# A two-layer hybrid decoder step: LayerNorm's subtraction on one engine, the recurrent state without its turn, far attention scores in residue order, and longer bank times in the plan of the passes

## The chip, the cores and the metric

The kernel runs on one core of one Trainium2 chip. The metric is the device time of one execution in microseconds (us). A core has TensorE (PE, matrix products, with its weight loads shown as PEld), VectorE (DVE), ScalarE (ACT), GpSimd (POOL) and SyncE (SP, which here only issues DMA transfers). Matrix products write to PSUM, which is used here as eight banks of 128 partitions x 512 float32 values; the other engines read it from there.

## The reference, cut to what matters

Two layers are applied to a prompt of 1024 positions and to 8 single decode positions. Each layer projects its input, splits the columns into an attention part (8 heads) and a recurrent RWKV-7 part (8 heads), joins both, and ends in two LayerNorms around a feed-forward part:

```python
def layer_norm(x, g, b):
    mu = xf.mean(-1, keepdims=True)
    var = jnp.square(xf - mu).mean(-1, keepdims=True)
    return (xf - mu) * lax.rsqrt(var + LN_EPS) * g + b

p   = x @ w_in
att = dilated_attention(q, k, v)       # (window, dilation) = (128,1), (512,4), (2048,16)
S   = S*w_t + (S @ a_t) b_t + v_t k_t  # RWKV-7 state, one step per position; y_t = S @ r_t
x1  = layer_norm(ALPHA*x + concat(att, rwk) @ w_out)
y   = layer_norm(ALPHA*x1 + square(relu(x1 @ w_up)) @ w_down)
```

The prompt's attention needs, for far keys, only positions whose distance is a multiple of 4. Outputs are the two results, the shifted rows, the final states, and the keys and values. All of it is float32.

## The kernel before

The prompt is worked on in two halves of 512 positions per layer; the second half carries the 8 decode columns too. A weight matrix product is computed as three products of a high and a low part (`dense_steps`, L389 to L391), each weight tile being split by ACT (L362) and DVE (L363).

The order of PE's instructions is written out ahead of time by a planner, `Streams`. Each stream is a generator that yields (cost, bank and how long it is held, latency until the next piece, bank it needs). The streams are, in order of priority, `s2` (the recurrence, `stage2`), `norm` (`normed`), `s1` (`stage1`), `att` (`attention`), `post`, `kv`, and last `dense`. In planned time, the first stream that is ready takes the next piece; `dense` fills the rest, and once entered it keeps PE for a while (`RUN`). The eight PSUM banks are divided by tag: `r` 1, `o` 2, `d` 3 (dense), `a` 2. The planned times decide the order alone: on the chip, semaphores decide. Other engines than PE keep an order that the framework makes.

**LayerNorm.** The last matrix product ahead of a LayerNorm (`out2` at L946, `down` at L1023) is computed in `passes`: eight row blocks o for the first 256 columns, then eight for the rest. A block is 12 matmuls of 256 columns, then DVE adds the bank into `t` (L952, L1028), and `ln.add` gathers sums and squares on DVE and POOL. `finish` (L750) makes the mean (L755), subtracts it from eight tiles at L759 (tiles 3 and 7 on DVE, the other six on POOL), makes the variance (L762, DVE at L763), and takes the inverse root on ACT. `scale` multiplies on DVE (L778). The first 256 columns are finished during the second eight blocks, the rest during the work that follows. There are 16 finishes. The last one ends the run.

**Recurrence.** `stage2` works on a unit of 256 positions of one pair of heads as four chunks; there are 32 units. After small solves it forms, per half c, products with `Pt` (L1365) and, over 128 rows, with `TV` (L1370: 64-column weights, 128 columns read). Then the chunks run in sequence: the incoming state `Z` is multiplied with `FG` (L1384, 128 columns), the part that is the new state is copied to `St` by DVE (L1386), turned by a product with a stacked identity (L1391, bank `r`), and scaled into the next `Z` by DVE (L1393). Each of these is a piece of its own.

**Gate.** `normed` makes the group norm of a unit in three pieces of tag `o`; where the decode columns come along (8 units), a further small product `pgd` (L1423) takes a bank of its own between the first and the second.

**Attention.** `att_load` stages q and k in two rotating buffers `stg` (L1544); ACT casts them (L1564, L1568) and POOL subtracts for the low parts (L1565, L1569). In the second half `qf` and `kf` are transferred straight from DRAM (L1556, L1557). `attention` computes for each of four query tiles and two heads the far scores (L1596) as four products, one per residue c, of 64 rows, 32 weight columns and 128 read columns; both operands are taken with a step of four elements. Then come the near scores (L1607, L1608).

Of the kernel before, what the change touches and what calls it, by code (L numbers as in the profile page):

```python
# [21 lines left out]
NB = 8  # L22
# [6 lines left out]
HB = T // 2  # L29
# [18 lines left out]
SWITCH = 280  # L48
SLK = (1.2, 2.2)
# [217 lines left out]
def body(ctx, tc, I, O):  # L267
# [130 lines left out]
    def dense(items, kts, xhh, xll, evac):  # L398

        res = []  # L400
        yield (0, None, 0, "d")
        yield from dense_steps(items, kts, xhh, xll, res)
        for it, p in zip(items, res):
            r = evac(it, p)
            if r is not None:
                yield r
        for i, it in enumerate(items):
            yield (res[-1] if i == 0 else 0, ("d", 900 + 500 * i), 0, None)
# [310 lines left out]
    class LayerNorm:  # L719
# [30 lines left out]
        def finish(self, c0, n, wait=0, spread=0):  # L750
            l, c = self.l, slice(c0, c0 + n)
            cm, s1, s2 = self.cm[:, c], self.s1[:, c], self.s2[:, c]
            yield (0, None, wait, "d")
            pm = bank("d", "lnm")
            PE.matmul(pm[:, :n], ones, s1, start=True, stop=True)  # L755
            A.activation(cm, pm[:, :n], AF.Copy, scale=1.0 / D)
            A.activation(s1, pm[:, :n], AF.Square, scale=1.0 / D)
            for k in range(8):
                (V if k % 4 == 3 else G).tensor_tensor(self.t[:, k, c], self.src(k, c0, n), cm, op=ALU.subtract)  # L759
            yield (860 * n / 512, ("d", 1300), 0, "d")  # L760
            pq = bank("d", "lnq")
# [104 lines left out]
    def half(l, h, prev=None):  # L866
# [82 lines left out]
        def out2(o, w, c0, nn):  # L949
            def ev(it, p):  # L950
                _, _, c0, n = it
                evs.append(V.tensor_tensor(src(o, c0, n), p[:, :n], src(o, c0, n), op=ALU.add))  # L952
            return dense([(w, 128, c0, nn)], K4, *acc(hs), ev)
# [70 lines left out]
        def down(o, w, c0, nn):  # L1024
            def ev(it, p):
                _, _, c0, n = it
                to = t[:, o, c0:c0 + n]
                evs.append(V.tensor_tensor(to, p[:, :n], to, op=ALU.add))  # L1028
            return dense([(w, 128, c0, nn)], K4, *acc(hs), ev)
# [281 lines left out]
    def stage2(l, h, p, u, s, st, Z, Zp):  # L1311
# [45 lines left out]
        for c in range(2):  # L1357
            pb = bank("o", f"pO{c}")
            o3 = pb.rearrange("p (b x) -> p b x", b=2)
            Oc.append(o3)  # L1360
            r = slice(64 * c, 64 * c + 64)
            for tb in range(2):
                for hd in range(2):
                    hs = slice(64 * hd, 64 * hd + 64)
                    PE.matmul(o3[hs, tb, 0:128], Pt[r, hd * 2 + tb, :], LB[r, hd, 2 * tb + c, 64 * c:64 * c + 128],  # L1365
                              start=(tb == 0), stop=True, skip_group_check=True)
            for tb in range(2):
                for hd in range(2):
                    hs = slice(64 * hd, 64 * hd + 64)
                    PE.matmul(o3[hs, tb, 128:256], TV[:, 2 * tb + c, hd, 0, :], LB[:, hd, 2 * tb + c, 64 * c:64 * c + 128],  # L1370
                              start=False, stop=True, skip_group_check=True)
            F4 = FG.rearrange("p (b c) x -> p c b x", c=2)[:, c]
            f0, g0 = 64 * (1 - c), 64 * c
            V.tensor_tensor(F4[:, :, f0:f0 + 64], AR[:, :, 320 * c:320 * c + 64], o3[:, :, f0:f0 + 64], op=ALU.subtract)
            V.tensor_tensor(F4[:, :, g0:g0 + 64], bc(istk, [(0, 2), (1, 64)]), o3[:, :, g0:g0 + 64], op=ALU.subtract)
            yield (960, None, 0 if c == 0 else 900, None if c == 0 else "r")
        note("lb", s)
        for cc in range(4):
            tb, c = divmod(cc, 2)
            o3 = Oc[c]  # L1380
# [31 lines left out]
    def normed(l, h, p, u, s, gup, gs):  # L1412
# [7 lines left out]
        if h == 1 and u == NU - 1:  # L1420
# [3 lines left out]
            V.tensor_copy(dd["gsd"][:, p, :], pz[:, 0:8])  # L1424
# [5 lines left out]
        pb = bank("o", "pgv")  # L1430
        PE.matmul(pb[:, 0:256], C("blk"), sq, start=True, stop=True)
# [103 lines left out]
    def att_load(l, h, p):  # L1535
# [39 lines left out]
    def attention(l, h, p, ops, vT, ahead):  # L1575
# [5 lines left out]
        for j in range(4):  # L1581
# [5 lines left out]
            Es = []  # L1587
            mx = ap_.tile([128, 12], F32, tag="mx", bufs=2, name="mx")
            for hd in range(2):
                hs = slice(64 * hd, 64 * hd + 64)  # L1590
                E = ap_.tile([128, 640], F32, tag="E", bufs=2, name="E")
                pS = bank("a", "pS")
                i, o = 2 * hd, 0
                if h == 1:
# [3 lines left out]
                    u0 = 32 * (7 - qt)  # L1598
                    far = (E[:, 0:128], pS[:, 0:128], C("far")[:, u0:u0 + 128], 1.0, -3e38, ALU.add, ALU.max,
                           mx[:, i:i + 1])  # L1600
                    i, o = i + 1, 128
                    if w > 384:
                        V.tensor_tensor_reduce(*far)
                        yield (300, ("a", 700), 0, "a")
                        pS, o = bank("a", "pS"), 0
                n = max(w, 256)
                PE.matmul(pS[:, o:o + n], qS[hd][:, ql:ql + 128], kS[hd][:, 128 * k0:128 * k0 + n], start=True, stop=False)  # L1607
                PE.matmul(pS[:, o:o + n], qL[hd][:, ql:ql + 128], kS[hd][:, 128 * k0:128 * k0 + n], start=False, stop=True)  # L1608
                if o > 0:
                    V.tensor_tensor_reduce(*far)  # L1610
# [3 lines left out]
                yield (n * 0.9 + 2.3 * o, ("a", 500 + w * 1.1 + o), 0, "a")  # L1614
# [5 lines left out]
                Es.append(E)  # L1620
# [282 lines left out]
```

## Time and profile before

| What | us |
|---|---|
| Median of three executions | 3280.85 (3280.17 to 3285.87) |
| Profiled execution, its own time | 3282.56 |
| Its span, first to last instruction | 3280.7 |
| PE busy in the span | 3130.2 |
| DVE, ACT, POOL busy | 2064.6, 1445.1, 983.3 |

The span is what the trace shows; the execution's own time lies 1.9 us above it. Mean granted clock of TensorE is 0.983 of its full 2.4 GHz. In the rows below a matmul on float32 operands stands as two records, so a count of 512 is 256 products. "Idle before" is the time in which an engine had nothing to do ahead of an instruction, with what ended it.

### The profile page before, as it was taken

The numbers are of one execution on the slowest core, as the hardware profiler recorded it, in microseconds if no ns is written. First come the engines' busy times: TensorE is split into PE (matmuls) and PEld (weight loads), VectorE is DVE, ScalarE is ACT, GpSimd is POOL, SyncE is SP. The second block draws the span as 40 slices with busy tenths as digits, with TensorE's granted clock in tenths as the row PEclk, the third lists the DMA queues.
The fourth block names the chain that finished last, engine by engine and source line by source line (L and its number), as shares of the span: only waits on it lengthen the run. The fifth ranks groups of instructions, "written<-read, shape, count | busy, mean of one in ns | idle before, by whom it ended". The sixth has DMA issues, their size and how long they took to land. (4 is left out here: it accounts for less than half of the span.)

```text
span 3280.7 us, 65951 instructions
## 1 busy us (share of the span) xinstructions
PE 3130.2 (95%) x24732; PEld 2656.7 (81%) x24732; DVE 2064.6 (63%) x4703; ACT 1445.1 (44%) x3266; POOL 983.3 (30%) x1841
## 2 busy tenths in 40 slices
PE   9999999899999999999999999998999999899998
PEld 7768887777777787788999999877767777889997
DVE  5666667855557476677665576568655664875556
ACT  4445454544433364454443345444434333543334
POOL 1443335521221134463121122456121201620012
PEclk9999999999999999999999999999999999999999
DMA  7544445344343355533333236543343434423332
GB/s 230 153 136 128 129 136 164 85 124 126 111 114 103 98 157 164 157 102 105 89 96 90 89 96 185 152 133 100 97 119 106 119 107 125 135 82 91 94 89 83
DMA packets 370503, 393.58 MB, mean 120 GB/s; under 512 B 145816, under 2 KB 223080, under 8 KB 370184
## 3 DMA queue, kind: packets, MB, share of 16 engines
q10 hardware_dynamic: 121152, 213.44, 22.0%
q1 hardware_dynamic: 249032, 175.93, 18.9%
q8 instruction: 195, 3.19, 0.4%
q14 instruction: 124, 1.02, 0.1%
HBM read 325.30 MB, written 63.97 MB: 119 GB/s over the span
## 5 line engine op out<-in xcount | busy, mean ns | idle before, releaser
L389 PE MATMUL dps<-xh,wh 128*128 128x256 f32 (+3 forms) x2984 | 974.1, 326 | 14.9 <-ACT wh L362 6.5
L390 PE MATMUL dps<-xl,wh 128*128 128x256 f32 (+3 forms) x2984 | 947.7, 318 | 11.0 <-DVE xl L781 8.0
L391 PE MATMUL dps<-xh,wl 128*128 128x256 f32 (+3 forms) x2984 | 943.8, 316 | 1.7 <-DVE wl L363 1.6
L362 ACT CAST wh<-wr 128x512 fp32r<-128x512 f32 (+1 forms) x772 | 474.6, 616 | 818.2 <-PE dps L390 759.5
L363 DVE TENSOR_TENSOR wl<-wr,wh 128x512 fp32r<-128x512 f32 (+1 forms) x772 | 579.5, 751 | 357.1 <-ACT wh L362 335.9
L389 PEld LDWEIGHTS dps<-xh,wh 128*128 128x128 f32 x2984 | 567.6, 190 | 75.9 <-issue 18.1
L390 PEld LDWEIGHTS dps<-xl,wh 128*128 128x128 f32 x2984 | 567.7, 190 | 49.1 <-DVE xl L781 12.2
L391 PEld LDWEIGHTS dps<-xh,wl 128*128 128x128 f32 x2984 | 567.4, 190 | 40.5 <-DVE wl L363 3.9
L389 PE MATMUL dps<-hh,wh 128*128 128x512 f32 (+2 forms) x1600 | 527.5, 330 | 9.1 <-ACT lnm L731 3.9
L390 PE MATMUL dps<-hl,wh 128*128 128x512 f32 (+2 forms) x1600 | 513.5, 321 | 3.5 <-DVE mx L1615 1.5
L391 PE MATMUL dps<-hh,wl 128*128 128x512 f32 (+2 forms) x1600 | 512.8, 321 | 0.0
L389 PEld LDWEIGHTS dps<-hh,wh 128*128 128x128 f32 x1600 | 304.4, 190 | 42.5 <-issue 9.6
L390 PEld LDWEIGHTS dps<-hl,wh 128*128 128x128 f32 x1600 | 304.7, 190 | 24.9 <-DVE hl L852 2.8
L391 PEld LDWEIGHTS dps<-hh,wl 128*128 128x128 f32 x1600 | 304.3, 190 | 22.9
L1234 POOL TENSOR_TENSOR tm<-BL,XB 32x15 f32<-32x15 f32 (+7 forms) x480 | 146.7, 306 | 394.2 <-DMA BL<-d_el 348.6
L995 DVE TENSOR_TENSOR t<-dps,t 128x256 f32<-128x256 f32 (+1 forms) x240 | 123.7, 516 | 165.3 <-PE dps L391 164.6
L1236 POOL TENSOR_TENSOR XB<-XB,tm 32x15 f32<-32x15 f32 (+7 forms) x480 | 156.6, 326 | 34.6
L748 POOL TENSOR_TENSOR ln<-ln,lsq 128x256 f32<-128x256 f32 (+1 forms) x112 | 90.8, 811 | 247.4 <-ACT lsq L746 243.4
L963 DVE CAST hh<-rl 128x256 fp32r<-128x256 f32 (+2 forms) x200 | 73.8, 369 | 96.3 <-ACT rl L962 93.2
L737 POOL TENSOR_TENSOR t<-t,ln 128x256 f32<-128x256 f32 (+1 forms) x32 | 27.8, 904 | 350.3 <-ACT ln L731 350.3
L961 ACT ACTIVATE rl<-dps 128x256 f32<-128x256 f32 (+2 forms) x200 | 88.3, 442 | 97.1 <-PE dps L391 90.5
L389 PE MATMUL dps<-hh,xh 128*128 128x256 f32 (+1 forms) x368 | 110.0, 299 | 13.2 <-DVE t L1028 5.8
(345 smaller groups left out, 5080.4 us busy)
## 6 DMA issues: line engine op xcount, KB each, us to landing
wr<-in_w_ff_up ACTq DMA_DIRECT2D x272, 256.0 KB
wr<-in_w_ff_down ACTq DMA_DIRECT2D x256, 256.0 KB
wr<-in_w_in ACTq DMA_DIRECT2D x220, 256.0 KB
stg<-d_qkv SPq DMA_DIRECT2D x128, 128.0 KB
wr<-in_w_out ACTq DMA_DIRECT2D x64, 256.0 KB
z<-d_z SPq DMA_DIRECT2D x24, 384.0 KB
d_qkv<-qe SPq DMA_DIRECT2D x128, 64.0 KB
kvc<-in_cache_k SPq DMA_DIRECT2D x32, 256.0 KB
```

The costliest lines, as they stand in the source:

```text
L362: self.copies.append(A.copy(h[:, :, :m], w[:, :, :m]))
L363: V.tensor_tensor(lo[:, :, :m], w[:, :, :m], h.bitcast(F32)[:, :, :m], op=ALU.subtract)
L389: PE.matmul(p[:m, :n], wh[:, wk % 4, :m], hi, start=(i == 0), stop=False)
L390: PE.matmul(p[:m, :n], wh[:, wk % 4, :m], lo, start=False, stop=False)
L391: PE.matmul(p[:m, :n], wl[:, wk % 4, :m], hi, start=False, stop=(i == last))
L737: G.tensor_tensor(t, t, self.cm[:, c0:c0 + n], op=ALU.subtract)
L748: G.tensor_tensor(s2, s2, sq, op=ALU.add)
L961: A.activation(r, p[:, :n], AF.Relu)
L963: V.tensor_copy(hh[:, c0:c0 + n], r)
L995: V.tensor_tensor(to, p[:, :n], to, op=ALU.add)
L1234: G.tensor_tensor(tv, bc(BL[:, 17 * j + 1:17 * j + 2], [(1, m), (0, j + 1)]), bc(XB[:, 16 * j:16 * j + 1], [(0, m), (1, j + 1)]), op=ALU.mult)
L1236: G.tensor_tensor(xv, xv, tv, op=ALU.add)
```

## The change

It has six parts. (1) `finish` subtracts the mean from all eight tiles on DVE. (2) `dense` takes the time that it holds a bank in the plan as an argument, and `out2` and `down` pass 2400 ns for the first column block and 4500 for the second in place of 900. (3) `stage2` computes the products with `TV` and `Z` in two halves of 64 columns; in one of them the operands trade places, so that the new state comes out turned already, and copy, turn and their bank are left out. The two halves c become one piece. (4) `normed` puts the decode columns' product in the third piece's bank. (5) `att_load` stages `qf` and `kf` through `stg`, and POOL copies them in residue order. (6) `attention` reads them side by side and makes the far scores of both heads together, alternating between the heads, in two banks.

```diff
+HOLD = (2400, 4500)
-    def dense(items, kts, xhh, xll, evac):
+    def dense(items, kts, xhh, xll, evac, hold=900):
...
-            yield (res[-1] if i == 0 else 0, ("d", 900 + 500 * i), 0, None)
+            yield (res[-1] if i == 0 else 0, ("d", hold + 500 * i), 0, None)
...
             for k in range(8):
-                (V if k % 4 == 3 else G).tensor_tensor(self.t[:, k, c], self.src(k, c0, n), cm, op=ALU.subtract)
+                V.tensor_tensor(self.t[:, k, c], self.src(k, c0, n), cm, op=ALU.subtract)
...
-            return dense([(w, 128, c0, nn)], K4, *acc(hs), ev)
+            return dense([(w, 128, c0, nn)], K4, *acc(hs), ev, HOLD[c0 > 0])
...
+        for c in range(2):
+            o3, f0, g0 = Oc[c], 64 * (1 - c), 64 * c
             for tb in range(2):
                 for hd in range(2):
                     hs = slice(64 * hd, 64 * hd + 64)
-                    PE.matmul(o3[hs, tb, 128:256], TV[:, 2 * tb + c, hd, 0, :], LB[:, hd, 2 * tb + c, 64 * c:64 * c + 128],
+                    PE.matmul(o3[hs, tb, 128 + f0:192 + f0], TV[:, 2 * tb + c, hd, 0, :], LB[:, hd, 2 * tb + c, 64:128],
+                              start=False, stop=True, skip_group_check=True)
+                for hd in range(2):
+                    hs = slice(64 * hd, 64 * hd + 64)
+                    PE.matmul(o3[hs, tb, 128 + g0:192 + g0], LB[:, hd, 2 * tb + c, 2 * g0:2 * g0 + 64], TV[:, 2 * tb + c, hd, 0, :],
                               start=False, stop=True, skip_group_check=True)
...
-            yield (960, None, 0 if c == 0 else 900, None if c == 0 else "r")
+        yield (1920, None, 900, None)
...
-                    PE.matmul(o3[hs, tb, 128:256], Z[hs, :], FG[hs, cc, :], start=False, stop=True, skip_group_check=True)
-            St = rp.tile([128, 64], F32, tag="St", bufs=2, name="St")
-            V.tensor_copy(St, o3[:, tb, 128 + 64 * c:192 + 64 * c])
-            yield (280, None, 900, "r")
-            pz = bank("r", "pz")
-            for hd in range(2):
-                hs = slice(64 * hd, 64 * hd + 64)
-                PE.matmul(pz[hs, 0:64], St[hs, :], istk[hs, :], start=True, stop=True)
+                    PE.matmul(o3[hs, tb, 128 + g0:192 + g0], FG[hs, cc, g0:g0 + 64], Z[hs, :], start=False, stop=True,
+                              skip_group_check=True)
+                for hd in range(2):
+                    hs = slice(64 * hd, 64 * hd + 64)
+                    PE.matmul(o3[hs, tb, 128 + f0:192 + f0], Z[hs, :], FG[hs, cc, f0:f0 + 64], start=False, stop=True,
+                              skip_group_check=True)
...
-            V.tensor_scalar(Z, pz[:, 0:64], Wd[:, cc, 64:65], None, op0=ALU.mult)
+            V.tensor_scalar(Z, o3[:, tb, 128 + g0:192 + g0], Wd[:, cc, 64:65], None, op0=ALU.mult)
             if cc < 3:
-                yield (130, ("r", 650), 900, None)
+                yield (280, None, 1000, None)
...
-            yield (860, ("o", 1000), 0, "o")
-            pz = bank("o", "pgd")
-            PE.matmul(pz[:, 0:8], gup, gs[:, UN:UN + NB], start=True, stop=True)
...
         pb = bank("o", "pgv")
+        if h == 1 and u == NU - 1:
+            PE.matmul(pb[:, 256:256 + NB], gup, gs[:, UN:UN + NB], start=True, stop=True)
...
-            S.dma_start(qf, d_qkv[l][1][p, 0])
-            S.dma_start(kf, d_qkv[l][0][p, 1])
+            for f, src, dst, at in ((qf, d_qkv[l][1][p, 0], inrow, byres),
+                                    (kf, d_qkv[l][0][p, 1], lambda t: t.rearrange("p (c k) -> p c k", c=4),
+                                     lambda t: t.rearrange("p (k c) -> p c k", c=4))):
+                t = ap_.tile([128, HB], F32, tag="stg", bufs=2, name="stg")
+                S.dma_start(t, src)
+                AQ.tensor_scalar(dst(f), at(t), 1.0, None, op0=ALU.mult)
...
-                    for c in range(4):
-                        PE.matmul(pS[32 * c:32 * c + 32, 0:128], qf[hs, ql + c:ql + 128:4], kf[hs, c:HB:4],
-                                  start=True, stop=True)
...
+                pSs = [bank("a", "pS") for _ in range(2)]
+                for c in range(4):
+                    for hd in range(2):
+                        hs = slice(64 * hd, 64 * hd + 64)
+                        PE.matmul(pSs[hd][32 * c:32 * c + 32, 0:128], qf[hs, ql + 32 * c:ql + 32 * c + 32],
+                                  kf[hs, 128 * c:128 * c + 128], start=True, stop=True)
```

## Rows read from the trace of the kernel before

**Rows 1.** The page's busy table: engine, busy us (share of span) xinstructions.

```profile
PE 3130.2 (95%) x24732; PEld 2656.7 (81%) x24732; DVE 2064.6 (63%) x4703; ACT 1445.1 (44%) x3266; POOL 983.3 (30%) x1841
```

**Rows 2.** Waits of PE: waiter <- releaser: us in total, times, longest us.

```profile
PE pgd L1423 <- ACT gs L1426: 11.3, 6, 4.1
...
PE pz L1391 <- DVE St L1386: 8.2, 3, 6.7
```

**Rows 3.** PE in order of time from 179.6: start, length in us, instruction.

```profile
179.62 0.39 PE L390 MATMUL dps<-xl,wh 128*128 128x512 f32 x1
179.85 0.40 PE L391 MATMUL dps<-xh,wl 128*128 128x512 f32 x1
180.18 0.33 PE L1391 MATMUL pz<-cst,St 64*64 64x64 f32 x4
180.44 0.50 PE L389 MATMUL dps<-xh,wh 128*128 128x512 f32 x1
180.78 0.39 PE L390 MATMUL dps<-xl,wh 128*128 128x512 f32 x1
```

**Rows 4.** Stretches: length, busy us of PE, PEld, DVE, ACT, POOL; clock, DMA.

```profile
1143.00:1179.00 36.00, 31.08 (x225) 28.98 (x225) 32.91 (x65) 21.83 (x51) 18.07 (x24) 0.95 0.31 90
2244.00:2290.00 46.00, 42.34 (x381) 37.70 (x380) 38.23 (x90) 19.58 (x49) 28.52 (x56) 0.93 0.24 66
```

**Rows 5.** PE's groups by line: xrecords | busy us, mean ns | idle us before.

```profile
L1391 PE MATMUL pz<-cst,St 64*64 64x64 f32 x512 | 43.0, 246 | 8.2 <-DVE St L1386 8.2
L1596 PE MATMUL pS<-kf,qf 64*32 64x128 f32 x512 | 42.9, 413 | 0.1
```

**Rows 6.** PE in order of time, the last turn that stands alone.

```profile
2685.90 0.33 PE L1391 MATMUL pz<-cst,St 64*64 64x64 f32 x4
```

**Rows 7.** PE in order of time, the product with the incoming state.

```profile
128.71 0.44 PE L1384 MATMUL pO<-FG,Z 64*64 64x128 f32 x4
129.08 0.44 PE L1607 MATMUL pS<-kS,qS 128*128 128x384 f32 x1
```

**Rows 8.** PE in order of time, the attention's far product with v.

```profile
510.32 0.64 PE L1662 MATMUL pof<-FT,vT 128*64 128x64 f32 x16
510.89 0.39 PE L389 MATMUL dps<-xh,wh 128*128 128x256 f32 x1
```

**Rows 9.** PE in order of time, the recurrence's local product.

```profile
119.00 0.66 PE L1370 MATMUL pO<-LB,TV 128*64 128x128 f32 x8
119.59 0.66 PE L1630 MATMUL pET<-cst,E 128*128 128x128 f32 x4
```

**Rows 10.** PE in order of time, the far scores and the decode's product.

```profile
442.34 0.67 PE L1596 MATMUL pS<-kf,qf 64*32 64x128 f32 x8
442.94 0.39 PE L1607 MATMUL pS<-kS,qS 128*128 128x256 f32 x1
...
857.04 0.64 PE L1818 MATMUL pdo<-kvc,dsc 128*32 128x128 f32 x16
857.62 0.50 PE L389 MATMUL dps<-xh,wh 128*128 128x512 f32 x1
```

**Rows 11.** Waits of ACT and POOL at the staged tiles; POOL's subtraction, ns min/median/max.

```profile
ACT kS L1568 <- DMA stg<-d_qkv: 44.9, 23, 4.1
...
POOL qL L1565 <- ACT qS L1564: 85.7, 23, 14.4
...
L1565 POOL TENSOR_TENSOR qL<-stg,qS x32: 1524/1556/1851, 84.8 to 2553.0; 128x512 fp32r<-128x512 f32 x32
```

**Rows 12.** DVE in order of time, the last finish.

```profile
3269.38 1.32 DVE L759 TENSOR_TENSOR t<-t,ln 128x264 f32<-128x264 f32 x2 [1.76 <-ACT ln L756]
...
3272.15 4.65 DVE L778 SCALAR_TENSOR_TENSOR t<-t,par,ln 128x264 f32<-128x264 f32 x8 [1.11 <-ACT ln L766]
```

**Rows 13.** DVE by line: durations in ns min/median/max, first and last start.

```profile
L747 DVE TENSOR_TENSOR ln<-ln,t x84: 405/427/4503, 592.7 to 3267.2; 128x256 f32<-128x256 f32 x66, 128x264 f32<-128x264 f32 x18
...
L778 DVE SCALAR_TENSOR_TENSOR t<-t,par,ln x128: 464/482/1030, 613.8 to 3276.3; 128x256 f32<-128x256 f32 x96, 128x264 f32<-128x264 f32 x32
```

More of the change, by code (lines that the diff above doesn't have):

```diff
@@ L1028, in ev @@
                 evs.append(V.tensor_tensor(to, p[:, :n], to, op=ALU.add))
-            return dense([(w, 128, c0, nn)], K4, *acc(hs), ev)
+            return dense([(w, 128, c0, nn)], K4, *acc(hs), ev, HOLD[c0 > 0])
         yield from passes(down, ln)
@@ L1357, in stage2 @@
         for c in range(2):
-            pb = bank("o", f"pO{c}")
-            o3 = pb.rearrange("p (b x) -> p b x", b=2)
+            o3 = bank("o", f"pO{c}").rearrange("p (b x) -> p b x", b=2)
             Oc.append(o3)
@@ L1369, in stage2 @@
                     hs = slice(64 * hd, 64 * hd + 64)
-                    PE.matmul(o3[hs, tb, 128:256], TV[:, 2 * tb + c, hd, 0, :], LB[:, hd, 2 * tb + c, 64 * c:64 * c + 128],
+                    PE.matmul(o3[hs, tb, 128 + f0:192 + f0], TV[:, 2 * tb + c, hd, 0, :], LB[:, hd, 2 * tb + c, 64:128],
[3 more added lines that the diff above has]
+                    PE.matmul(o3[hs, tb, 128 + g0:192 + g0], LB[:, hd, 2 * tb + c, 2 * g0:2 * g0 + 64], TV[:, 2 * tb + c, hd, 0, :],
                               start=False, stop=True, skip_group_check=True)
             F4 = FG.rearrange("p (b c) x -> p c b x", c=2)[:, c]
-            f0, g0 = 64 * (1 - c), 64 * c
             V.tensor_tensor(F4[:, :, f0:f0 + 64], AR[:, :, 320 * c:320 * c + 64], o3[:, :, f0:f0 + 64], op=ALU.subtract)
             V.tensor_tensor(F4[:, :, g0:g0 + 64], bc(istk, [(0, 2), (1, 64)]), o3[:, :, g0:g0 + 64], op=ALU.subtract)
-            yield (960, None, 0 if c == 0 else 900, None if c == 0 else "r")
+        yield (1920, None, 900, None)
         note("lb", s)
@@ L1379, in stage2 @@
             tb, c = divmod(cc, 2)
-            o3 = Oc[c]
+            o3, f0, g0 = Oc[c], 64 * (1 - c), 64 * c
             if Z is not None:
@@ L1419, in normed @@
         V.scalar_tensor_tensor(y, pb[:, 0:256], -1.0 / 64, y, op0=ALU.mult, op1=ALU.add)
-        if h == 1 and u == NU - 1:
-            yield (860, ("o", 1000), 0, "o")
-            pz = bank("o", "pgd")
-            PE.matmul(pz[:, 0:8], gup, gs[:, UN:UN + NB], start=True, stop=True)
-            V.tensor_copy(dd["gsd"][:, p, :], pz[:, 0:8])
         gg = gs[:, 0:256]
@@ L1430, in normed @@
         pb = bank("o", "pgv")
+        if h == 1 and u == NU - 1:
+            PE.matmul(pb[:, 256:256 + NB], gup, gs[:, UN:UN + NB], start=True, stop=True)
+            V.tensor_copy(dd["gsd"][:, p, :], pb[:, 256:256 + NB])
         PE.matmul(pb[:, 0:256], C("blk"), sq, start=True, stop=True)
@@ L1586, in attention @@
             ql = j * 128
-            Es = []
+            Es, pSs, far = [], [], []
             mx = ap_.tile([128, 12], F32, tag="mx", bufs=2, name="mx")
             for hd in range(2):
[L1590 to L1594, printed above, removed]
-                    for c in range(4):
-                        PE.matmul(pS[32 * c:32 * c + 32, 0:128], qf[hs, ql + c:ql + 128:4], kf[hs, c:HB:4],
-                                  start=True, stop=True)
[L1598 to L1606, printed above, removed]
+                Es.append(ap_.tile([128, 640], F32, tag="E", bufs=2, name="E"))
@@ new lines, in attention @@
+            if h == 1:
+                yield (0, None, 0, ("a", 2))
+                pSs = [bank("a", "pS") for _ in range(2)]
+                u0 = 32 * (7 - qt)
+                for c in range(4):
[3 more added lines that the diff above has]
+                                  kf[hs, 128 * c:128 * c + 128], start=True, stop=True)
+                for hd in range(2):
+                    far.append((Es[hd][:, 0:128], pSs[hd][:, 0:128], C("far")[:, u0:u0 + 128], 1.0, -3e38, ALU.add, ALU.max,
+                                mx[:, 2 * hd:2 * hd + 1]))
+                if w > 384:
+                    for hd in range(2):
+                        V.tensor_tensor_reduce(*far[hd])
+                    yield (0, ("a", 700), 0, None)
+                    yield (300, ("a", 900), 0, "a")
+                    pSs, far = [], []
@@ L1607, in attention @@
+            n = max(w, 256)
+            o = 128 if far else 0
+            for hd in range(2):
+                E, i = Es[hd], 2 * hd + h
+                pS = pSs[hd] if far else bank("a", "pS")
                 PE.matmul(pS[:, o:o + n], qS[hd][:, ql:ql + 128], kS[hd][:, 128 * k0:128 * k0 + n], start=True, stop=False)
                 PE.matmul(pS[:, o:o + n], qL[hd][:, ql:ql + 128], kS[hd][:, 128 * k0:128 * k0 + n], start=False, stop=True)
-                if o > 0:
-                    V.tensor_tensor_reduce(*far)
+                if far:
+                    V.tensor_tensor_reduce(*far[hd])
@@ L1613, in attention @@
                                        mx[:, i - 1:i] if h else -3e38, ALU.add, ALU.max, mx[:, i:i + 1])
-                yield (n * 0.9 + 2.3 * o, ("a", 500 + w * 1.1 + o), 0, "a")
+                yield (n * 0.9 + 1.2 * o, ("a", 500 + w * 1.1 + o), 0, "a" if hd == 0 and not far else None)
                 V.tensor_scalar(mx[:, 4 + hd:5 + hd], mx[:, i:i + 1], -0.125, None, op0=ALU.mult)
@@ L1619, in attention @@
                 V.tensor_scalar(E[:, :f + w], E[:, :f + w], mx[:, 8 + hd:9 + hd], None, op0=ALU.mult)
-                Es.append(E)
             if j == 3:
```

## The prediction

> **What bounds the kernel now.** I read the busy table first. TensorE (PE) is busy 3130.2 of the 3280.7 us span, VectorE (DVE) 63%, and GpSimd (POOL) 30% [rows 1]. So PE is the bound, and there are two ways to gain: give it less to do, or end one of its waits, which together are 3280.7 - 3130.2 = 150 us. The view of who waited for whom says how these are spread. The largest entry is 11.3 us in six waits, and the one for the state's copy, 8.2 in three, comes a few lines down [rows 2]. The reader should see that no single wait carries the run.
>
> A PE row's length is not its price, since matmuls overlap. The price is the distance from one start to the next, read from the time-ordered PE rows. Dense rows of 512 columns follow each other in 0.23 us. Around a small group the distance grows. Before the turn of the state at 180.18 it is 0.33 (179.85 to 180.18), and after the turn the first dense row holds 0.34 (180.44 to 180.78) [rows 3]. So one trip from dense work to small work and back costs about 0.10 + 0.11 = 0.2 us beside the small work itself.
>
> Last I read the table by stretches for the LayerNorm passes. In the pass at 1143 only dense work runs, and DVE is busy 32.91 of 36.00 us, PE 31.08. There DVE sets the pace. In the pass at 2244 other streams fill in (381 matmul records against 225), and PE idles 46.00 - 42.34 = 3.7 us [rows 4]. Going by the code and the record counts, three of the eight passes are of the second kind, so about 11 us of idle time lie in them.
>
> **The change part by part.** The sum is made against the profiled execution, 3282.56 us (span 3280.7 and 1.9 around it), which lies 1.7 above the median of 3280.85.
>
> *The state is not turned.* The 512 records of the turn [rows 5] are groups of four (two matmuls, two records each), so 128 groups. Each occupies 0.26 us (180.18 to 180.44) [rows 3]. 128 x 0.26 = -33 us, all of it PE time.
>
> *Fewer pieces.* A unit's tail falls from ten pieces to five. Of the 128 turns, 27 stand alone between dense rows, the first at 180.18 [rows 3], the last at 2685.90 [rows 6]: 27 x 0.2 = -5. The other 101 share their trip with other streams, and up to 101 x 0.2 = 20 could go. I take a quarter, -5, because the other streams' work still has to enter somewhere. Together -10 (bounds -5 and -25).
>
> *The product with the incoming state in halves.* It exists 120 times (128 less the 8 first chunks without a state). Now it is four records of 128 columns in 0.37 us (128.71 to 129.08) [rows 7]. Then it is eight of 64. As two separate groups like the turn's that is 0.52. For a second group that follows at once, the nearest row is the far product with v, whose sixteen 64-column records take 0.57 us (510.32 to 510.89), 0.036 each [rows 8]. 0.26 + 4 x 0.036 = 0.40, so +0.03 x 120 = +4 (bounds: 8 x 0.036 = 0.29, -10; 0.52, +18).
>
> *The local product in halves.* Now it is eight records of 128 columns in 0.59 us (119.00 to 119.59) [rows 9], 64 times. Then it is sixteen of 64 columns with 128 rows and 64 columns of weights, which is the form of rows 8: 0.57. I take 0. The far end is the isolated price of 0.26 for four: 1.04 a time, 64 x 0.45 = +29.
>
> A rule of the Trainium skill speaks against both halvings. TensorEngine Tiling (Array Packing), section Instruction Overhead, gives every matmul about 60 cycles of overhead. By it, as an estimate, 240 + 256 = 496 more matmuls at 25 ns would cost 12 us and the whole sum would be -63. Rows 8 and 9 disagree, since half the columns there cost half the time. Either result lies in the forecast's own range.
>
> *Far scores by residue.* Eight records of 128 columns, read with a step of four, take 0.60 us (442.34 to 442.94). The decode's product, also 32 columns of weights and 128 read columns but side by side, has sixteen in 0.58 (857.04 to 857.62) [rows 10]. That is 0.075 against 0.036 a record. The 512 records [rows 5] at 0.039 less give -20. I take the nearest row's price as it stands. The ends are 0 (the step is not what costs) and -25 (the two heads, on different rows of the array, overlap too).
>
> *What the residue order costs.* Eight loads of q and k (layers x head pairs, second half only) pass two more tiles through the two staging buffers, and POOL copies each. A copy is one input of 128x512; a POOL subtraction of that size took 1.56 us [rows 11]. 16 x 1.56 = 25 us at most on an engine that is busy for a third of the time. But the first q tile's transfer on SyncE's queue now waits for a buffer that POOL must empty, and behind it stand all later loads of that queue. ScalarE (ACT), which casts the tile, waits too, and behind ACT stand weight casts and the relu that PE needs. ACT already waits for staged tiles 23 times, 44.9 us, 4.1 at the longest [rows 11]. I take +5: eight loads, 4 us more each, a sixth of it reaching PE, because the load for the next pair starts well ahead of its first use. Ends: 0, and 8 x 4.1 = +33.
>
> *The gate's last columns ride in the next bank.* The six waits of 11.3 us [rows 2] are for ACT's copy that frees a bank the piece no longer takes. -11 (0 if the wait moves to the next group, where ACT is just as late). The eight groups themselves stay.
>
> *The copy of the state.* Its 128 DVE copies go, and with them the 8.2 us wait [rows 2]. The state's scaling is next in line and inherits part. -4 (bounds -8, and +5 if it is later than the copy was).
>
> *DVE alone subtracts the mean.* At the end of the run two subtractions on DVE, beside POOL's six, take 1.32 us, 0.66 each [rows 12]; DVE's add over the same size in the sum alone has a median of 0.427 [rows 13]. So eight on DVE in a row are 3.4 us instead of 1.32. What follows gains. Eight scalings took 4.65 there, while POOL was still subtracting [rows 12], against a median of 0.482 alone [rows 13], 3.9. At the run's end this chain is all there is: +2.1 - 0.8 = +1.3 us. The other fifteen finishes have the same balance or a better one, and part of it lies under PE work. I take +1 and, for all fifteen, 0. The bounds are 15 x 1.3 = +20 where nothing covers it, and -8 if POOL's freed time helps its other streams.
>
> *Banks held longer in the model.* HOLD changes no instruction, only the planner's order. Above c0 = 0 a bank counts as free 4.5 us after its block. Two blocks of the other banks cover about 2.8 (2 x 12 rows of 256 columns, each at half of the 0.23 us of a 512-column row [rows 3]), so the planner looks for 1.7 us of other work per block. In the three passes with such work, about 11 us of PE idle time can be filled, at one more trip of 0.2 per block (24 blocks, +5). I take -4 (bounds -11 and +5). In the other five passes there is nothing to insert.
>
> *Clock.* In the pass at 2244 the granted clock is 0.93 and at 1143 0.95 [rows 4], that is, some of that time at 1.2 instead of 2.4 GHz, after PE had idled. Fewer waits leave fewer such stretches: -3 (0 to -8).
>
> Sum: -33 - 10 + 4 + 0 - 20 + 5 - 11 - 4 + 1 + 0 - 4 - 3 = -75. From the median, 3280.85 - 75 = **3206 us**.
>
> **The rivals.**
> *Half of it comes back as waits.* PE gets 75 us less to do, but the dense stages then run closer to DVE and ACT, whose work hardly shrinks, and in the passes DVE is already ahead of PE [rows 4]. For it: ACT's and POOL's queues stand in order behind late transfers [rows 11]. Against it: outside the passes DVE has a third of its time free [rows 1]. At half, 3281 - 38 = 3243.
> *More than the sum.* The trips fall by the whole 25, the far scores by 25, the halves at the incoming state by 10, and the fill in the passes by 11: -75 - 15 - 5 - 14 - 7 = -116, 3165. It needs every bound at its good end; halfway, 3185, is more credible.
> *Slower: the staging chain.* POOL is in order. When its copy of the q tile stands behind one of its waits for ACT, the buffer stays full, SyncE's queue stands, ACT waits for the tile and PE for ACT. POOL's waits of this kind reach 14.4 us [rows 11]. Eight loads at 14.4, all passed on to PE, are 115 us: 3206 + 110 (the sum held 5 already) = 3316. It decides from (75 + 5) / 8 = 10 us per load. Against it: no ACT wait for a staged tile was longer than 4.1 [rows 11].
> *The change does not do what it says.* The far scores keep 0.075 a record, and the halves cost what isolated groups cost (+18 + 29 - 4): -75 + 20 + 43 = -12, nearly even, 3269. Within 0.2%, about 6.5 us, it would need a little more, such as the bank wait staying.
>
> **How the numbers follow.** Forecast (3188 to 3226) 0.55; half comes back (3226 to 3262) 0.20; more than the sum (below 3188) 0.14; no gain to speak of (3262 to 3287) 0.06, of which 0.04 within 0.2%; slower 0.05. The time is that of the likeliest, 3206. For 8 in 10 the range takes the forecast, most of the half case and most of the better one: 3172 to 3250. About 0.2% is what a measurement of this kernel can tell from no change. Faster by more 0.91, within it 0.04, slower by more 0.05.
>
> **What would show it.** The turn's records are gone, and eight records of the incoming product lie at 0.40 us. The local product stays at 0.59 for sixteen. Far scores at or below 0.30 per eight. No PE wait stands at the gate's columns. In the pass at 1143 DVE does eight subtractions in 3.4 us and PE's idle time is unchanged; in those with other work it is lower. PE's busy time falls by some 50 to 60 us. What would make it wrong: ACT waits for staged tiles well above 45 us in all, PE waits for weight casts that were not there, small groups priced by count instead of by columns, or a PE idle time that grows as its busy time falls.

## The result and the profile after

The changed kernel took 3236.3 us (median; 3232.2 to 3244.7) against 3280.5 of the kernel before: ratio 0.9866, 95% interval 0.9842 to 0.989. That is 44 us less, where the forecast was 75 less. The direction is right, and the range (3172 to 3250) holds the time, but it lies among the times of the rival that half of the gain comes back as waits (3226 to 3262, given 0.20), and not in the forecast's own range.

The page of the profiled execution (3244.69 us, the slowest of the four, 8 us above their median), span and busy table, as [rows 1]:

```profile
span 3242.9 us, 66797 instructions
...
PE 3054.3 (94%) x25212; PEld 2651.7 (82%) x25212; DVE 2034.9 (63%) x4671; ACT 1439.2 (44%) x3266; POOL 930.1 (29%) x1761
```

Two numbers tell the story. PE's busy time fell by 3130.2 - 3054.3 = 75.9 us. Its idle time rose from 3280.7 - 3130.2 = 150.5 to 3242.9 - 3054.3 = 188.6, by 38.1. The span's 37.8 is the difference. The work went as forecast or better, and the waits gave about half of it back (by the median, which is 44 us less, a little under half).

First the work, PE in order of time in the profile after (start, length, instruction), of the same kinds as [rows 7, 9, 10]:

```profile
118.39 0.68 PE L1365 MATMUL pO<-LB,Pt 64*64 64x128 f32 x16
119.00 0.34 PE L1372 MATMUL pO<-LB,TV 128*64 128x64 f32 x4
...
125.70 0.33 PE L1389 MATMUL pO<-Z,FG 64*64 64x64 f32 x4
125.87 0.28 PE L1393 MATMUL pO<-FG,Z 64*64 64x64 f32 x4
126.08 0.66 PE L1664 MATMUL po<-ET,vT 128*64 128x128 f32 x8
...
249.68 0.34 PE L1372 MATMUL pO<-LB,TV 128*64 128x64 f32 x4 [1.06 <-ACT TV L1354]
...
250.55 0.29 PE L1376 MATMUL pO<-TV,LB 128*64 128x64 f32 x4
250.77 0.66 PE L698 MATMUL pqt<-cst,qe 128*128 128x128 f32 x4
...
435.38 0.45 PE L1603 MATMUL pS<-kf,qf 64*32 64x128 f32 x16
435.76 0.39 PE L1619 MATMUL pS<-kS,qS 128*128 128x256 f32 x1
```

Read the distance from a group's start to the next group's. The product with the state takes 0.38 (125.70 to 126.08), against 0.37 before. The local product takes 1.09 for both halves c (249.68 to 250.77; its first and last rows are shown), against two times 0.59. The far scores of both heads take 0.38, against two times 0.60. The products with `Pt` of both halves take 0.61 (118.39 to 119.00). In the kernel before, one half took 0.58, twice a unit:

```profile
117.25 0.65 PE L1365 MATMUL pO<-LB,Pt 64*64 64x128 f32 x8
117.83 0.66 PE L1370 MATMUL pO<-LB,TV 128*64 128x128 f32 x8
```

Then the waits of PE (in total, times, longest us), as [rows 2]:

```profile
PE dps L391 <- DVE xl L782: 11.9, 20, 1.6
PE pgm L1420 <- ACT y L1401: 11.1, 9, 2.3
PE pET L1641 <- DVE E L1631: 8.8, 3, 6.5
PE pgv L1432 <- ACT gq L1426: 8.7, 3, 4.5
PE pO L1389 <- DVE Z L1396: 8.5, 8, 2.0
...
PE pgv L1432 <- DVE gsd L1431: 5.6, 5, 3.3
```

The first is of dense work and was there before (8.0, at the same place). The five below it are of small pieces. Before, the state's scaling had 5.5, the gate's product (pgv, for gq) 1.4, and the other three did not stand in the list. Summed over PE's groups, idle time fell in dense work from 55.6 to 49.0 us, and rose in the group norm and gate (pgm, pgd, pgv) from 12.7 to 26.6 and in attention from 6.2 to 28.2. The groups of attention (xrecords | busy us, mean ns | idle us before):

```profile
L1641 PE MATMUL pET<-cst,E 128*128 128x128 f32 x336 | 58.7, 291 | 10.0 <-DVE E L1631 8.8 <-DVE bv L1276 0.9 <-ACT TV L1268 0.3
...
L1619 PE MATMUL pS<-kS,qS 128*128 128x256 f32 (+2 forms) x128 | 51.5, 409 | 7.6 <-DVE ao L1666 4.1 <-ACT LB L1256 3.1 <-POOL kS L1574 0.4
...
L1673 PE MATMUL pof<-FT,vT 128*64 128x64 f32 x256 | 11.0, 231 | 4.3 <-ACT FT L1657 4.3
```

With 3.4 at the far scores and 2.9 at the product with v, these make 28 us. Of the 8.8 us at L1641, 6.5 are a single wait, inside the LayerNorm pass at 2229. First PE's row, then three of DVE's ahead of it:

```profile
2274.75 0.69 PE L1641 MATMUL pET<-cst,E 128*128 128x128 f32 x2 [6.51 <-DVE E L1631]
```

```profile
2256.25 1.76 DVE L760 TENSOR_TENSOR t<-t,lnm 128x256 f32<-128x256 f32 x5
...
2262.54 2.16 DVE L779 SCALAR_TENSOR_TENSOR t<-t,par,ln 128x256 f32<-128x256 f32 x4
...
2274.29 0.41 DVE L1631 TENSOR_SCALAR E<-E,mx 128x384 f32<-128x384 f32 x1
```

DVE shows no idle time between 2256 and 2274. The softmax of both heads stands there in line behind LayerNorm's subtractions and scalings and the recurrence's operands, and PE waits for the last step of it.

### The profile page after: what moved, and what is told of

Read it like the earlier page. It is cut to its first block, busy times and chain, and to the rows that moved or that the text cites. A ratio compares the mean times of both kernels' runs of the same rounds, so it can differ in the third digit from the quotient of the medians.

```text
span 3242.9 us, 66797 instructions
## 1 busy us (share of the span) xinstructions
PE 3054.3 (94%) x25212; PEld 2651.7 (82%) x25212; DVE 2034.9 (63%) x4671; ACT 1439.2 (44%) x3266; POOL 930.1 (29%) x1761
## 5 line engine op out<-in xcount | busy, mean ns | idle before, releaser
L1235 POOL TENSOR_TENSOR tm<-BL,XB 32x15 f32<-32x15 f32 (+7 forms) x480 | 156.1, 325 | 386.0 <-DMA BL<-d_el 297.2
L738 POOL TENSOR_TENSOR t<-t,lnm 128x256 f32<-128x256 f32 (+1 forms) x80 | 69.6, 903 | 245.6 <-ACT lnm L732 230.7
```

Source lines behind the costliest of these rows:

```text
L738: G.tensor_tensor(t, t, self.cm[:, c0:c0 + n], op=ALU.subtract)
L1235: G.tensor_tensor(tv, bc(BL[:, 17 * j + 1:17 * j + 2], [(1, m), (0, j + 1)]), bc(XB[:, 16 * j:16 * j + 1], [(0, m), (1, j + 1)]), op=ALU.mult)
```

## The experiments

Two theories stood against each other: that the *plan's fill* (bank times that send small work into the LayerNorm passes) brings the waits, and that the *shorter recurrence* does. The later runs are about the far scores and about how much the order alone moves. PE's busy and idle time are given from each run's page, idle as span less busy.

**The state's part alone (state_only).** The kernel before with the changes of `stage2` only, as in part 3 of the change.

> The kernel before with the third part of the change alone (products in halves, no turn of the state). Priced by the trace after: the recurrence's slots on PE fall by about 50 us (293 to 244) and the trips to small work by some 7, so PE's busy time falls by 50 to 57. Theory 'the plan's fill brings the waits' (the longer bank times send small work into the LayerNorm passes, where DVE is late): no new waits here, 3281 - 55 = about 3226. Theory 'the shorter recurrence brings its own waits' (group norm and next solves now follow sooner than the engines beside PE can serve): PE's waits rise by 15 to 30 us here already, about 3240 to 3255.

Measured: 3228.0 us, ratio 0.9829 (0.981 to 0.9849). Its page:

```profile
span 3228.0 us, 66798 instructions
...
PE 3071.5 (95%) x25212; PEld 2650.4 (82%) x25212; DVE 2035.0 (63%) x4575; ACT 1441.7 (45%) x3266; POOL 972.7 (30%) x1841
```

Busy time is down by 58.7 us and idle time up by 6.0, to 156.5. The shorter recurrence brings hardly any waits in sum; some moved (its list stands at the later group norm below). This part alone gives 55 us. That is 8 us more than the whole change by the medians and 12 by the ratios, with intervals that just overlap, so the other five together gained nothing and probably cost some 10.

**Bank times as before (hold900).**

```diff
-HOLD = (2400, 4500)
+HOLD = (900, 900)
```

> The whole change, but banks are held 900 ns in the plan in all passes, as before. In the trace after, the three passes that have other work hold 20.6 us of PE gaps against 10.4 before, and 17 us of lost clock against 9. 'The plan's fill brings the waits': these go back, 15 to 20 us faster than the change, about 3218. 'The recurrence brings its own waits': the fill is worth what it was made for (dense gaps of 9.3 fell to 1.1), so without it the time is the same or up to 8 us more, 3236 to 3244.

Measured: 3231.9 us, 0.9849 (0.9826 to 0.9872). This overlaps the change's interval and meets neither expectation: the waits do not go back (idle 181.2), nor is the fill worth anything that shows. In the pass with other work at 2229, the trace of the whole change shows what the fill meets (columns as in [rows 4]):

```profile
2229.00:2287.00 58.00, 48.77 (x473) 43.65 (x473) 42.88 (x113) 28.31 (x75) 25.35 (x49) 0.91 0.24 70
```

More small work lies in the pass (473 records), but PE idles 9.2 us, where the stretch of rows 4 had 3.7. The wait of 6.5 us for DVE shown above is most of it. Without the fill it is still 5.3 us.

**LayerNorm's subtractions back on POOL (ln_split).**

```diff
-                V.tensor_tensor(self.t[:, k, c], self.src(k, c0, n), cm, op=ALU.subtract)
+                (V if k % 4 == 3 else G).tensor_tensor(self.t[:, k, c], self.src(k, c0, n), cm, op=ALU.subtract)
```

> The whole change, but six of LayerNorm's eight subtractions are on POOL again; the plan is the same to the piece. The prediction's step (DVE alone is neutral but for the run's end, where it costs 1.3): the same within 5 us. If DVE's burst is what makes the small work in the passes wait: up to 20 us faster, about 3216. If the shared time of DVE and POOL is what the change cured: 10 us or more slower, 3246.

Measured: 3243.0 us, 0.9882 (0.9861 to 0.9903), 0.0016 above the change, inside both intervals. DVE's burst is not what makes small work wait, since without it idle time is 190.8 and the wait in the pass is 6.5 us as before.

**Far scores with a step of four, unstaged (far_step4).** The order of PE's work is that of the change.

```diff
-                S.dma_start(t, src)
-                AQ.tensor_scalar(dst(f), at(t), 1.0, None, op0=ALU.mult)
+            S.dma_start(qf, d_qkv[l][1][p, 0])
+            S.dma_start(kf, d_qkv[l][0][p, 1])
...
-  qf[hs, ql + 32 * c:ql + 32 * c + 32], kf[hs, 128 * c:128 * c + 128]
+  qf[hs, ql + c:ql + 128:4], kf[hs, c:HB:4]
```

> The whole change, but q and k of the far scores come straight from DRAM and are read with a step of four again; heads still alternate, the plan is the same. The step costs: the 64 groups of eight go from 0.21 back to about 0.60, +24 us, about 3260. The staging costs time elsewhere (the slow rival): less than that, and ACT's waits for staged tiles fall by 10 us or more. Alternating the heads is what made it cheap: PE's time for the far scores stays near 14 us and the run is the same.

Measured: 3225.3 us, 0.9822 (0.9799 to 0.9845). It is 11 us faster than the change by the medians, with intervals that just overlap. The second expectation comes nearest: ACT's waits fell by more than 10 us. But it allowed for a loss smaller than 24 us, and this is a gain. PE in order of time in this run:

```profile
451.38 0.69 PE L1599 MATMUL pS<-kf,qf 64*32 64x128 f32 x16
452.01 0.39 PE L1615 MATMUL pS<-kS,qS 128*128 128x256 f32 x1
```

Sixteen records with the step take 0.63 when the heads alternate. Before, eight took 0.60 [rows 10]. So the alternation is worth 0.075 - 0.039 = 0.036 a record, and reading side by side another 0.039 - 0.024 = 0.015, 8 us over 512 records. (No run reads side by side without alternating, so this split holds for that order alone.) In PE's total the 8 us don't show: it is 3052.1 here and 3054.3 in the change. Against them stand the waits. ACT's for staged tiles, first in the change, then in this run:

```profile
ACT kS L1573 <- DMA stg<-d_qkv: 40.2, 18, 4.6
...
ACT qS L1569 <- DMA stg<-d_qkv: 31.1, 17, 5.4
```

```profile
ACT kS L1569 <- DMA stg<-d_qkv: 36.0, 17, 4.1
...
ACT qS L1565 <- DMA stg<-d_qkv: 19.9, 11, 5.4
```

They are 15 us shorter without the two extra tiles, and PE's idle time is 168.3 in place of 188.6 (of two executions that lie 22 us apart, where the medians differ by 11). Attention has little part in that: its idle time is 25 us here against 28. The wait of PE that differs most is for a load of the recurrence, issued from SyncE as the staged tiles are, first in the change, then here:

```profile
PE pT L1309 <- DMA X<-d_el: 8.0, 5, 4.0
```

```profile
PE pT L1309 <- DMA X<-d_el: 0.9, 2, 0.7
```

It is 6.3 to 15.0 us in the six kernels that stage the two tiles, and at most 5.1 in the eight that don't.

**The copies on DVE (far_dve).**

```diff
-                AQ.tensor_scalar(dst(f), at(t), 1.0, None, op0=ALU.mult)
+                V.tensor_copy(dst(f), at(t))
```

> The whole change, but DVE makes the two residue-order copies in place of POOL; PE's work and plan are the same. On POOL a copy took 2.0 us and stood behind 16.8 us of waits for PE to finish reading the old tiles. If POOL's late and slow copies hold the staging buffers and through them ACT's casts: ACT's waits for staged q tiles fall from 31 us towards 20, and the run comes most of the way to the unstaged 3225. If it is the two extra tiles in the row of transfers itself, whoever copies: the same as the change, 3236, or slower where DVE now stands still for PE.

Measured: 3249.1 us, 0.9891 (0.9868 to 0.9913). A copy is shorter (on average 0.63 to 0.76 us against 2.1), yet the run is no faster than the change, and ACT's waits for staged tiles add up to the same (71.5 us, 71.3 in the change). So POOL's slowness is not the cause. What is left is that two more tiles pass through the two staging buffers, whoever copies; that is concluded by exclusion. Against far_step4, with the same order of PE's work, the intervals lie apart.

**Far scores as before (far_old).** The whole change without the diffs of `att_load` and `attention`.

> The whole change without its parts 5 and 6: far scores one head after the other, read with a step of four straight from DRAM, with the plan's steps of before for attention. PE's slots for the far scores go back from 14 to 38 us. If making both heads' scores at once is what lets attention wait (its gaps on PE were 6 us before, 28 after, 25 with step four and alternating heads, 10 with the state's part alone), those gaps fall to about 10, and with the staging's 11 us gone the run is 3236 + 25 - 18 - 11 = about 3232. If the waits come from the shorter recurrence and the fill, the gaps stay near 25: 3236 + 25 - 11 = 3250.

Measured: 3227.1 us, 0.9819 (0.98 to 0.9838). PE's busy time is 25.2 higher than in the change (3079.5), its idle time 41.8 lower (146.8). Attention's groups in this run:

```profile
L1631 PE MATMUL pET<-cst,E 128*128 128x128 f32 x336 | 56.7, 286 | 0.1
...
L1608 PE MATMUL pS<-kS,qS 128*128 128x256 f32 (+2 forms) x128 | 53.3, 418 | 4.3 <-DVE mx L1613 2.8 <-DVE ao L1656 1.3
```

With 2.2 at the product with v, attention's idle time is 6.6 us against 28. The first of the two expectations holds: parts 5 and 6 together save 25 us of PE and lose more than that in waits. Staging is not all of the loss. Against far_step4, which has the alternating heads and no staging (0.9822), this run is level (0.9819), though it keeps PE 27 us longer. Nor do ACT's waits for staged tiles explain it: they are 69 us here, without the two tiles.

**The order alone (switch300).** `SWITCH = 300` in place of 280 in the planner; every instruction is the same.

> The whole change with the planner's price of a return to dense work at 300 in place of 280 ns: no instruction is added, taken away or resized, only the order shifts here and there. It measures how far a reshuffled order alone moves the time. If differences of 5 us between the other runs mean something: within 4 us of 3236. If the order's luck decides them: 6 to 15 us to either side.

Measured: 3243.2 us, 0.9877 (0.9858 to 0.9895), 0.0011 or 4 us from the change by the ratios, inside both intervals. Single waits move more than the sum: attention's idle time is 36 us against 28.

**A later group norm (norm_late, state_late).** The first on the whole change, the second on the state's part alone, without the second hunk.

```diff
-        yield (0, None, 900, "o")
+        yield (0, None, 1800, "o")
         pb = bank("o", "pgm")
...
-            V.tensor_copy(dd["gsd"][:, p, :], pb[:, 256:256 + NB])
         PE.matmul(pb[:, 0:256], C("blk"), sq, start=True, stop=True)
+        if h == 1 and u == NU - 1:
+            V.tensor_copy(dd["gsd"][:, p, :], pb[:, 256:256 + NB])
```

> The whole change with two delays in the group norm: its first product is planned 1800 ns after the unit's end in place of 900, and the copy of the gate's decode columns is issued behind the second product, not ahead of it. In the trace after, PE waited 11.1 us for the unit's copy there (before: none of the longer waits), 5.6 us for the gate's copy. 'The shorter recurrence sends the norm too early': both waits go and the gaps of the norm fall from 27 to about 12, 3236 - 15 = about 3221. 'Waits only move': the same within 5 us, with the gaps back at other groups.

> The state's part alone, with the norm's first product planned 1800 ns after the unit in place of 900. The state's part alone gave 3228, with 9.5 us of PE waiting for the unit's copy by ACT at that product. If the shorter recurrence sends the norm too early: that wait falls below 4 and the run to about 3220. If waits only move: 3224 to 3232.

Measured: norm_late 3223.7 us, 0.9817 (0.98 to 0.9834), 16 us better than the change. state_late 3242.0 us, 0.9871 (0.9848 to 0.9895), 14 us worse than state_only. The waits of PE in state_only, then in state_late:

```profile
PE pn L1170 <- ACT sg L569: 11.6, 7, 4.4
PE pgm L1419 <- ACT y L1400: 9.5, 4, 4.4
```

```profile
PE pn L1170 <- ACT sg L569: 17.0, 9, 4.4
...
PE pT L1308 <- DVE mx L1620: 7.6, 1, 7.6
...
PE pgm L1419 <- ACT y L1400: 0.3, 1, 0.3
```

The wait that was aimed at is gone, 9.5 to 0.3, and PE's idle time rose all the same, from 156.5 to 173.8, at other groups. state_late is slower than both its expectations. So the delay that came with a gain of 16 us in one kernel came with a loss of 14 in another. I had taken the early norm for the cause of the waits; that theory falls. The two edits are not the same, though: norm_late also has the later copy of the gate's columns. In the change that copy stands between two products on one bank, and PE waits 5.6 us for it (gsd, above); in norm_late this wait is gone. Whether the copy, the delay or the order gained the 16 us was not separated. best1 below, where the delay alone is added, is no faster either.

**The parts that paid (state_far4, state_far4_ln, best1).** First the state's part with the alternating heads, unstaged as in far_step4; then DVE alone on the mean in addition; best1 has the later norm on top.

> The kernel before with the state's part and the alternating heads alone; q and k of the far scores unstaged and read with a step of four; LayerNorm, bank times and gate as before. The state's part alone gave 3228; alternating took PE's far slots from 38 to 22 us. If parts add: 3228 - 17 = about 3211. If both heads at once bring attention waits (about 15 us): 3226, no gain. If the alternation's gain is eaten by the plan and more: above 3230.

> The run with the state's part and the alternating, unstaged heads (3216.6, ratio 0.9795), and DVE alone on LayerNorm's mean in addition; the plan is the same to the piece. Putting the subtractions back on POOL in the whole change cost 0.0016 of the ratio, some 5 us, within both intervals. If that is a real gain of less contention between DVE and POOL: 0.978, about 3211. If LayerNorm's subtraction is neutral and the 5 us were scatter: 0.979 to 0.981. The run with a later norm in addition had 0.9808; if that was the later norm's doing and not LayerNorm's, this one lies below it.

> The kernel before with those parts that paid: the state without its turn, DVE alone on the mean, both heads' far scores alternating but unstaged with a step of four, and the norm's first product planned 1800 ns after the unit. Bank times and gate as before. If the parts add as their runs say: 3216 (state and far heads) - 6 (LayerNorm) - 8 (norm) = about 3202. If reshuffling and waits elsewhere take it back: 3212 to 3220.

Measured: 3216.6 us, 0.9795 (0.9777 to 0.9814); 3211.4 us, 0.978 (0.9759 to 0.9801); 3221.3 us, 0.9808 (0.9785 to 0.9832). The first lies between its expectations of 3211 and 3226: against state_only it gains 11 us by the medians, with intervals that just overlap, so alternating unstaged heads probably pays in this order, while far_step4 was level with far_old. The second came out as its first expectation said, but its interval also holds the other. best1 missed both of its expectations: with the later norm it is 9 us slower by the ratios than state_far4_ln, with intervals that overlap. state_far4_ln is the best kernel found, 0.9866 - 0.978 = 0.0086 or 28 us ahead of the change, with intervals apart. Its page:

```profile
span 3206.6 us, 66777 instructions
...
PE 3050.1 (95%) x25212; PEld 2644.7 (82%) x25212; DVE 2023.4 (63%) x4671; ACT 1436.7 (45%) x3266; POOL 899.2 (28%) x1745
```

PE is as busy as in the change (3054.3) and idles 156.5 in place of 188.6 us.

## Why the prediction was half right

**The state's turn and the trips (-33, -10), right in kind and too small.** The state's part took 58.7 us off PE's busy time, where the terms for turn, trips and halves sum to -39. I had not priced that the products with `Pt` of both halves c would stand next to each other: sixteen records take 0.61 (118.39 to 119.00) where a unit had two times 0.58, so 32 units save 17.6 us, and their busy time by line fell from 41.9 to 21.8 us. With the 3 us of the local product (1.09 against 1.18 a unit) that is the difference of 20.

**The halves (+4 and 0), right.** 0.38 against the forecast 0.40, and 1.09 for thirty-two records of the local product, 0.54 for sixteen, against 0.57. By the overhead that the Trainium skill gives each matmul (TensorEngine Tiling (Array Packing), Instruction Overhead), these groups would have grown, since they have twice the matmuls. The trace does not agree for these shapes: they take 0.38 against 0.37 and 1.09 against 1.18.

**Far scores (-20), right in size, its reason only in part.** The saving on PE is 25 us, the good end of the range. Alternating the heads alone gives 18 of it (512 x 0.036), which the prediction listed only as the far end of the bound; reading side by side adds 8 on top. What it gives without alternating, the term's own case, no run shows.

**Staging (+5), the step that was most mis-sized.** With the same order of PE's work it is the difference between far_step4 and the change: 11 us by the medians, 14 by the ratios, although the change saves 8 us of PE there. So it cost 11 to 14 us net, and about 20 with those 8, as idle time shows too (188.6 against 168.3). The sum was 8 x 4 us of ACT's delay, a sixth of it for PE. ACT's delay came out smaller, 15 us, and PE's loss larger than all of it. So the sixth is the part that failed: what PE lost did not come through ACT's wait for these tiles alone. The load of the recurrence, issued on the same queue, accounts for 7 us; the path of the rest is not shown. I also read the wait before too low. The 44.9 us of rows 11 are kS alone, and the kernel before has a second line:

```profile
ACT qS L1564 <- DMA stg<-d_qkv: 14.3, 9, 3.9
```

Together ACT waited 59.2 us for staged tiles, against 71.3 in the change. That rise, and PE's idle time growing while its busy time fell, are two of the signs that the prediction gave for being wrong.

**Both heads at once: a term that was missing.** The prediction costed no wait for it. Attention's idle time went from 6.6 (far_old) to 28 us, and is 25 without the staging (far_step4). It is 15 to 36 us in all ten kernels that make both heads' scores at once, and 6 to 10 in the four that don't, so it comes with this part of the change in every order that was run. Why is shown for one wait only: 6.5 us for DVE's scaling of the exponentials (L1631), which stands behind other work in DVE's row. That the two heads' softmax coming in one burst makes the rest is argued; it was not tried by itself.

**The gate's wait (-11), wrong.** It moved to the next group, as the bound's end of 0 had it: 8.7 + 5.6 = 14.3 us at L1432, where 1.4 had been. The 5.6 are of this part's own making. In state_only, where the gate is as before, the wait at pgd is already gone, so there was nothing left for this part to remove. **The state's copy (-4), right.** Its wait of 8.2 us is gone, and the one for the scaling rose from 5.5 to 8.5, so 5.2 are gained.

**LayerNorm (+1), about right.** The eight subtractions take 2.84 us, where 3.4 were forecast. DVE in order of time at the end of the run, as [rows 12]:

```profile
3231.55 2.84 DVE L760 TENSOR_TENSOR t<-t,ln 128x264 f32<-128x264 f32 x8 [1.23 <-ACT ln L757]
3234.31 0.43 DVE L764 SCALAR_TENSOR_TENSOR ln<-lnq,ln 128x264 f32<-128x264 f32 x1
3235.78 3.32 DVE L779 SCALAR_TENSOR_TENSOR t<-t,par,ln 128x264 f32<-128x264 f32 x8 [1.04 <-ACT ln L767]
```

From the first subtraction to the last scaling it takes 7.55 us (3231.55 to 3239.10), against 7.42 before (3269.38 to 3276.80): +0.1, not +1.3, since the scalings without POOL beside them fell from 4.65 to 3.32. Two pairs of runs with the same order (ln_split and the change, state_far4 and state_far4_ln) both put DVE alone about 5 us ahead. Each lies within its intervals, so this is likely and not shown.

**Bank times (-4), no gain to be seen.** hold900 is level with the change. In the pass at 2229 PE's dense work waits 0.3 us, where it waited 2.2 in rows 4's stretch, as planned, but the small work that fills it waits in turn for DVE (6.5 us), which has LayerNorm's work in line.

**Clock (-3), wrong in sign.** The mean granted clock fell from 0.983 to 0.974. PE idled more, not less, and more of the time was at 1.2 GHz: in the pass at 2229 the granted clock was 0.91, against 0.93 in rows 4.

**The sum.** Terms for work came to -59 and measured -76. Terms for waits and clock came to -16 and measured +38. The rival "half comes back" had the size right. It looked for the cause in dense stages, whose idle time fell; the rise is 22 us at attention and 14 at the group norm and gate. Its mechanism, work that meets a busy DVE in the passes, shows only in the one wait of 6.5 us. That the range holds the time is in part luck. The work saved 17 us more than its terms, for a reason that the sum did not have; without these 17 the run would lie at an estimated 3253, outside the range. What stays open: state_far4_ln and far_step4 differ in the bank times, the gate and the order they give (0.978 against 0.9822, 14 us); which of the three it is was not settled. Nor is it known how far an order alone moves the time: switch300 shows 4 us, which is inside the noise, and the later norms (-16, +14) change more than the order.

## What to carry to other kernels

Where PE is 95% busy, work taken off it can be summed from the distances between starts. Here most of the terms held, and the sum fell 17 us short because a neighbour was left out: look also at what the edit puts next to each other. Waits can't be summed so. One that is removed can come back at the next piece, as the gate's did, and a delay that removed a wait of 9 us came with a run 14 us slower. An operand rearranged to read faster has to be charged for its path, the buffers and transfers that it takes from others, before the gain on PE is counted.

## What the runs showed of the hardware

Products on different rows of the array ran side by side when they were neighbours. Far scores of two heads (64 rows each), issued in turn, took 0.63 us for sixteen records with the same step-of-four reads that took 0.60 for eight of one head. The products with `Pt` of two halves, one on either 64 rows, took 0.61 for sixteen records, where eight of one half took 0.58. With the heads alternating, the step of four costs less than the prediction took: 0.039 against 0.024 us a record. And eight scalings by LayerNorm on DVE took 3.32 us with no subtraction on POOL beside them, against 4.65 before.
